# A block kernel whose first modulation third is loaded and multiplied ahead of its token rows

## The chip, the cores and the metric

The kernel runs on one core of a Trainium2 chip, as one program. The metric is its device time in microseconds (us); lower is better. A measurement is several executions, and their median is told.

## The reference, cut to what matters

The program is one layer of a diffusion transformer: 1024 tokens and 256 context tokens of width 1024. A modulation vector of six parts, computed from a conditioning vector, shifts and scales the normed tokens; a mixing block (gated linear attention beside a long convolution, the "hyena" part) and a mixture of 16 experts follow.

```python
mod_x = split((silu(c) @ w_ada + b_ada), N_MOD)            # six parts of 1024
mod_c = split((silu(c_ctx) @ w_ada + b_ada), N_MOD)
def project(h, mod):
    p = (rmsnorm(h, norm_mix_g) * (1 + mod[1]) + mod[0]) @ w_in
    ...
def hyena_filters(L, w1, b1, w2, b2, w3, freq):
    hdn = sin(freq * (z @ w1 + b1)); hdn = sin(freq * (hdn @ w2 + b2))
    h = (hdn @ w3).reshape(L, 2, 2, 512) * exp(-t * deltas)
    ...
x = x + mod_x[2] * merge(gla(project(x)), hyena(project(x), filters))
x = x + mod_x[5] * moe(rmsnorm(x) * (1 + mod_x[4]) + mod_x[3])
return rmsnorm(x, norm_final_g)
```

Parts 0 and 1 of the modulation (the shift and the scale of the first norm) are its first third: without them no token row can be projected.

## The kernel before, in words

The weight matrix w_ada of the modulation is 1024 by 6144. It is taken in three thirds `t` of 2048 columns. Of each third, 16 tiles `wt` of 128 rows by 1024 columns (512 KB) are loaded, and each is multiplied by four matmul instructions in the program (eight on the engine) with a 32-column tile `sc` of the two conditioning vectors (`mod_piece`, L325 to L336). The four write four quarters of 32 partitions of one accumulator `pm`; the sum is added into the tile `mo`, which holds the bias (`mod_begin`, L318 to L324). The two vectors stand in the rows 32 g and 32 g + 1 of `mo`, for the four column groups g. Thirds 1 and 2 are computed much later, among the convolution's slots, and are written to the DRAM tensor `d_mod` (`mod_end`). The first third stays on the chip: four transposes (L349) turn it into per-channel columns `mcol`, and `g1` is its scale with the norm's gain.

The order of the program at the start is this. The features of the filters are computed first: two small layers with sines (`sin_layer`; products L243 and L254, activation L236), with the loads of the filters' output weights `w3raw` ahead of them and a split of each of these into a high and a low part (`split_w3`, ACT L247 and DVE L248). Then come the DFT matrices `fmat` and `fneg`, and the first four tiles of token rows (`rows_of`, 128 rows each): loads of the rows and of the position table's parts (L282, L288, L295), their additions on VectorE (L297, L298), a square on ScalarE for the norm (L300), and the scaling (L305). Then the first third of the modulation, all 16 tiles in one piece. After that `columns` transposes and modulates the rows (L501, L503) into `xh` and `xl`, for the first four row tiles and then for the second four. The second four have the position table added by an accumulating transfer that GpSimd issues (L290), and use the same buffers as the first four. The filters (`filter_front`, products L451 and L452, multiplication L454; `filter_mid`, the transform's products L467 and L468) are eight units without any need of the rows; the projections (`short_conv`, product L542) need both halves of the rows.

What each engine does when is set at build time: a planner takes the instructions in program order as their priority, and puts each on its engine's queue when, by its own estimate, its inputs are there. So the filters' products stand between those of the modulation and of the rows. On the chip each queue is in order. The SyncE queue (SP) issues nearly all loads, also in that order; a load waits where its buffer isn't free. The modulation's tiles of the first third have eight buffers (tag `wa`) in a pool that is closed before the pool of `xh` and `xl` is opened.

## Time and profile before

| | |
|---|---|
| median of 3 runs | 1385.44 us |
| lowest and highest | 1383.4 and 1390.76 us |
| the profiled execution's own time | 1382.24 us |
| its span | 1380.5 us |
| TensorE busy | 1275.1 us |
| VectorE busy | 1149.6 us |

The page gives one execution: engine sums, 40 slices, groups and waits. Engines: PE is TensorE's matmuls, PEld its weight loads, DVE is VectorE, ACT is ScalarE, POOL is GpSimd, SP is SyncE, which only issues transfers. A timeline row has the start in us, the duration, the engine, the line, the operation with its output and inputs, and a count; in brackets, the idle time of the engine before it and what ended it. Where a row counts "x2" or "x8", the duration is that of the whole row. The chain of waits that ended last is followed back only to about 650 us in this profile, so that the start must be read from windows, waits and timelines.

### The profile page before, as it was taken

The page shows a single profiled execution, that of the slowest core. Times are in us where ns is not written, and L with a number is a line of the kernel's source. Part 1 is how long each engine was busy: PE and PEld are TensorE (multiplying, and loading weights), DVE is VectorE, ACT ScalarE, POOL GpSimd, SP SyncE. Part 2 cuts the span into 40 slices and gives each one's busy share as a digit, 9 for nine tenths or more (in the row PEclk, how much of TensorE's full clock was granted, in tenths as well). Part 3 has the DMA queues.
Part 4 walks back from the last instruction along what each step waited for, and adds up shares of the span by engine and source line. Part 5 has one row for each costly group of instructions (what it writes and reads, how often), then busy time and mean ns, then how long its engine had stood idle before and what let it go on. Part 6 is the DMA issues. An engine that isn't in the chain of part 4 may idle for free.

```text
span 1380.5 us, 21546 instructions
## 1 busy us (share of the span) xinstructions
PE 1275.1 (92%) x7720; PEld 1043.0 (76%) x7720; DVE 1149.6 (83%) x1920; ACT 806.4 (58%) x1228; POOL 130.1 (9%) x142
## 2 busy tenths in 40 slices
PE   6978999999999997987996899999999999999982
PEld 4777888687898896766775678888888888877762
DVE  6877838899778778878756799999999999988885
ACT  3247453211221415885553578888888888877864
POOL 1110000010100110000000000011111111012010
PEclk9998999999999998998996799999999999999996
DMA  7893541774655536766668689999999999999765
GB/s 223 315 241 118 177 128 47 229 218 146 187 169 167 154 100 186 176 158 174 221 230 348 241 316 357 358 394 381 395 381 390 385 389 383 372 366 370 265 204 223
DMA packets 154362, 354.81 MB, mean 257 GB/s; under 512 B 28389, under 2 KB 74013, under 8 KB 153999
## 3 DMA queue, kind: packets, MB, share of 16 engines
q1 hardware_dynamic: 134911, 292.84, 59.7%
q0 software_dynamic: 19344, 60.61, 15.7%
q8 instruction: 60, 0.98, 0.3%
q14 instruction: 47, 0.39, 0.1%
HBM read 310.89 MB, written 50.89 MB: 262 GB/s over the span
## 4 chain that ended last, share of the span: by engine, by line
PE 45%; DVE 4%; DMA 2%; issue 1%; ACT 1%; SPq 0%; POOLq 0%; POOL 0%; DVEq 0%; ACTq 0%
PE pex L151 13%; PE pex L152 12%; PE pex L150 12%; PE ptx L1341 2%; DVE elo L147 1%; PE psel L1252 1%; PE pout L150 1%; DMA eraw<-w_up 1%; PE pout L151 1%; DVE xf L1414 1%; PE pout L152 1%; DVE state L635 0%; PE po L1123 0%; PE po L1127 0%; DMA xs<-d_h,ix 0%
## 5 line engine op out<-in xcount | busy, mean ns | idle before, releaser
L147 DVE TENSOR_TENSOR elo<-eraw,ehi 128x1024 fp32r<-128x1024 f32 x256 | 302.5, 1219 | 13.0 <-issue 5.9
L151 PE MATMUL pex<-elo,thi 128*128 128x512 f32 x768 | 306.0, 398 | 4.7 <-DVE elo L147 4.4
L150 PE MATMUL pex<-ehi,thi 128*128 128x512 f32 x768 | 305.4, 398 | 2.3 <-ACT thi L144 1.3
L152 PE MATMUL pex<-ehi,tlo 128*128 128x512 f32 x768 | 303.4, 395 | 0.8 <-DVE tlo L147 0.8
L144 ACT ACTIVATE ehi<-eraw 128x1024 fp32r<-128x1024 f32 x256 | 265.0, 1068 | 50.2 <-PE pex L152 49.3
L151 PEld LDWEIGHTS pex<-elo,thi 128*128 128x128 f32 x768 | 145.2, 189 | 40.4 <-DVE elo L147 10.4
L150 PEld LDWEIGHTS pex<-ehi,thi 128*128 128x128 f32 x768 | 145.2, 189 | 34.1 <-ACT thi L144 1.7
L152 PEld LDWEIGHTS pex<-ehi,tlo 128*128 128x128 f32 x768 | 145.0, 189 | 31.7 <-DVE tlo L147 1.2
L147 DVE TENSOR_TENSOR elo<-erawl,ehi 128x1024 fp32r<-128x1024 f32 x128 | 149.4, 1218 | 6.4 <-ACT ehi L144 5.6
L144 ACT ACTIVATE ehi<-erawl 128x1024 fp32r<-128x1024 f32 x128 | 131.3, 1057 | 19.6 <-PE pex L152 18.0
L144 ACT ACTIVATE whi<-wraw 128x1024 fp32r<-128x1024 f32 x30 | 31.8, 1060 | 104.9 <-DMA wraw<-w_in 28.4
L542 PE MATMUL phy<-xh,whi 128*128 128x512 f32 x192 | 77.2, 402 | 11.3 <-ACT whi L144 11.3
L543 PE MATMUL phy<-xl,whi 128*128 128x512 f32 x192 | 76.0, 396 | 0.0
L150 PE MATMUL pvg<-whi,xh 128*128 128x256 f32 x256 | 73.2, 286 | 0.0
L151 PE MATMUL pvg<-wlo,xh 128*128 128x256 f32 x256 | 72.4, 283 | 0.0
L152 PE MATMUL pvg<-whi,xl 128*128 128x256 f32 x256 | 72.4, 283 | 0.0
L1387 POOL DMA_INDIRECT d_acc<-y,ix x15 | 34.6, 2308 | 392.5 <-DVE y L1386 392.5
L1346 ACT ACTIVATE tt<-ptx,fcol,gfcol 128x128 f32<-128x128 f32 x128 | 48.7, 463 | 33.9 <-PE ptx L1341 33.9
L545 PE MATMUL phy<-xh,wlo 128*128 128x512 f32 x192 | 61.9, 399 | 0.0
L438 ACT ACTIVATE D<-pdft 128x512 f32<-128x512 f32 x32 | 19.1, 597 | 68.9 <-PE pdft L468 39.4
L147 DVE TENSOR_TENSOR wlo<-wraw,whi 128x1024 fp32r<-128x1024 f32 x30 | 36.6, 1221 | 21.2 <-ACT whi L144 21.1
L467 PE MATMUL pdft<-kk,fmat 128*128 128x128 f32 x256 | 52.1, 286 | 0.3 <-ACT D L438 0.2
(452 smaller groups left out, 2596.3 us busy)
## 6 DMA issues: line engine op xcount, KB each, us to landing
eraw<-w_gate SPq DMA_DIRECT2D x128, 512.0 KB
eraw<-w_up SPq DMA_DIRECT2D x128, 512.0 KB
erawl<-w_down SPq DMA_DIRECT2D x128, 512.0 KB
wt<-w_ada SPq DMA_DIRECT2D x48, 512.0 KB
wraw<-w_in SPq DMA_DIRECT2D x30, 512.0 KB
kspec<-d_spec SPq DMA_DIRECT2D x16, 512.0 KB
xt<-x SPq DMA_DIRECT2D x8, 512.0 KB
d_spec<-ue POOLq DMA_DIRECT2D x8, 512.0 KB, 5.9
```

What stands on the lines that cost most here:

```text
L144: A.activation(hi, src, AF.Copy)
L147: V.tensor_sub(lo, src, hi.bitcast(F32))
L150: T.matmul(out_, lh, rh, start=first, stop=False)
L151: T.matmul(out_, lh, rl, start=False, stop=False)
L152: T.matmul(out_, ll, rh, start=False, stop=last)
L467: T.matmul(ps[:, r], fmat[:, r, m1], kk[m1 // 4][:, 0, m1 % 4], start=True, stop=False)
L542: T.matmul(ps[:, h], hi[:, k], rh[k][:, h], start=k == 0, stop=False)
L543: T.matmul(ps[:, h], hi[:, k], rl[k][:, h], start=False, stop=False)
L545: T.matmul(ps[:, h], lo[:, k], rh[k][:, h], start=False, stop=k == KT - 1)
L1341: T.transpose(pt[:, k], src[:, (4 * g + k) * P:(4 * g + k + 1) * P], ident)
L1346: A.activation(tt[:, k], pt[:, k], AF.Identity, bias=fcol[:, 0, kk_:kk_ + 1], scale=gfcol[:, kk_:kk_ + 1])
L1387: G.indirect_dma_start(out=d_acc[:, :], out_offset=bass.IndirectOffsetOnAxis(ap=ix[:, :1], axis=0), in_=y, in_offset=None, compute_op=ALU.add)
```

## The change

The conditioning vector's activation, the helpers of the modulation and the first half of the first third (`mod_piece(0, (0, 1), ...)`, eight tiles) move ahead of the loads of `w3raw`. The second half (`mod_piece(0, (2, 3), ...)`) stays after the second `w3raw` split and the first decay, but now stands ahead of the first token rows, which move behind the transposes of the modulation and `g1`. The first third has 16 buffers instead of eight, so no load of it waits. Since it is two pieces, there are two accumulators and two additions into `mo`. In all three thirds the bias comes in two transfers of four partitions (every 32nd) instead of eight of one, and in the last two the vectors go out in two instead of four.

```diff
     SY.dma_start(ccol[:, :, 1], io["c_ctx"].rearrange("(k p) -> p k", p=P))
+    V.tensor_scalar(fb[:, 3:4], fb[:, 2:3], 1.0 / (2 * math.pi), None, op0=ALU.mult)
+    sc = early.tile([P, KT, 32], F32, name="sc")
+    G.memset(sc, 0.0)
+    A.activation(sc[:, :, 0:2], ccol, AF.Silu)
...
+    def mod_columns(rows, t, i):
+        return rows[i, 2048 * t:2048 * t + 2048].rearrange("(h g j) -> g h j", h=2, g=4)
+
+    def mod_begin(t, pool):
+        mo = pool.tile([P, 512], F32, name="mo", tag="mo", bufs=1)
+        G.memset(mo, 0.0)
+        for i in range(2):
+            SY.dma_start(mo[i::32].rearrange("g (h j) -> g h j", h=2), mod_columns(io["b_ada"], t, 0))
+        return mo
...
+    def mod_end(t, mo):
+        for i in range(2):
+            G.dma_start(mod_columns(d_mod, t, i), mo[i::32].rearrange("g (h j) -> g h j", h=2))
+
+    mo = mod_begin(0, early)
+
+    def wa(shape, name):
+        return wap.tile(shape, F32, name=name, tag="wa", bufs=16)
+
+    mod_piece(0, (0, 1), mo, wa)
 
     w3v = io["hy_w3"][0].rearrange("k (o d c) -> o k d c", o=2, d=2)
...
-    first_rows = rows_of(io["x"][0], 0, 4, True)
...
-    def mod_columns(rows, t, g):
-        return rows[:, 2048 * t:2048 * t + 2048].rearrange("r (h g j) -> r g h j", h=2, g=4)[:, g]
...
-        for g in range(4):
-            for i in range(2):
-                SY.dma_start(mo[32 * g + i:32 * g + i + 1].rearrange("r (h j) -> r h j", h=2), mod_columns(io["b_ada"], t, g))
...
-        for g in range(4):
-            G.dma_start(mod_columns(d_mod, t, g), mo[32 * g:32 * g + 2].rearrange("r (h j) -> r h j", h=2))
...
-    mo = mod_begin(0, early)
-    mod_piece(0, range(4), mo, lambda shape, name: wap.tile(shape, F32, name=name, tag="wa", bufs=8))
+    mod_piece(0, (2, 3), mo, wa)
     gcol = early.tile([P, KT], F32, name="gcol")
...
         V.scalar_tensor_tensor(g1[:, i], mcol[:, i, 1], 1.0, gcol, op0=ALU.add, op1=ALU.mult)
+
+    first_rows = rows_of(io["x"][0], 0, 4, True)
+
     wa_stack.close()
```

## Rows read from the trace of the kernel before

**Rows 1.** The page, its span and the sums of the engines.

```profile
span 1380.5 us, 21546 instructions
...
PE 1275.1 (92%) x7720; PEld 1043.0 (76%) x7720; DVE 1149.6 (83%) x1920; ACT 806.4 (58%) x1228; POOL 130.1 (9%) x142
```

**Rows 2.** Windows: us, busy of PE, PEld, DVE, ACT, POOL, granted clock, DMA share, GB/s.

```profile
0.00:20.60 20.60, 7.89 (x8) 2.16 (x8) 11.97 (x25) 4.96 (x8) 3.29 (x10) 1.00 0.80 223
...
28.00:46.00 18.00, 18.00 (x154) 17.16 (x154) 15.44 (x29) 6.97 (x14) 1.55 (x3) 1.00 0.75 282
46.00:73.50 27.50, 27.50 (x264) 19.48 (x264) 20.16 (x46) 6.06 (x7) 3.73 (x7) 1.00 0.85 256
73.50:95.90 22.40, 22.29 (x192) 21.60 (x191) 22.06 (x52) 12.56 (x21) 6.27 (x9) 1.00 0.90 256
95.90:107.20 11.30, 0.04 (x1) 0.00 (x0) 2.97 (x8) 4.41 (x9) 0.00 (x0) 0.72 0.91 240
107.20:111.00 3.80, 3.76 (x15) 3.57 (x16) 3.68 (x12) 0.66 (x3) 0.54 (x1) 0.50 0.34 138
```

**Rows 3.** Waits of PE, 20 to 200 us: total, times, longest.

```profile
PE phy L542 <- ACT whi L144: 11.3, 1, 11.3
```

**Rows 4.** Timeline, SP's loads of the second rows and ACT's queue behind them.

```profile
82.86 1.85 SPq L288 DMA_DIRECT2D xt<-x  x4
...
105.09 1.06 ACT L300 ACTIVATE jk<-xt 128x1024 bf16<-128x1024 f32 x1 [2.35 <-DMA xt<-c_pos]
...
106.14 1.04 ACT L144 ACTIVATE whi<-wraw 128x1024 fp32r<-128x1024 f32 x1
```

**Rows 5.** DMA queues, 84 to 106 us: packets, MB, share of 16 engines.

```profile
q0 software_dynamic: 892, 3.14, 61.2%
```

**Rows 6.** Timeline of PE, the filters' first products.

```profile
20.65 0.58 PE L451 MATMUL pw<-w,h2h 128*128 128x256 f32 x1 [3.50 <-ACT h2h L266]
...
22.39 0.41 PE L452 MATMUL pw<-w,h2l 128*128 128x256 f32 x1
22.61 0.41 PE L451 MATMUL pw<-w,h2h 128*128 128x256 f32 x1
...
28.16 0.63 PE L467 MATMUL pdft<-kk,fmat 128*128 128x128 f32 x2
...
30.09 0.28 PE L452 MATMUL pw<-w,h2l 128*128 128x256 f32 x1
30.21 0.28 PE L451 MATMUL pw<-w,h2h 128*128 128x256 f32 x1
```

**Rows 7.** Timeline of PE, one piece of the modulation between transform products.

```profile
46.77 0.39 PE L468 MATMUL pdft<-kk,fmat 128*128 128x128 f32 x2
47.08 0.64 PE L334 MATMUL pm<-wt,sc 128*32 128x256 f32 x8
47.65 0.49 PE L467 MATMUL pdft<-kk,fmat 128*128 128x128 f32 x2
47.98 0.39 PE L468 MATMUL pdft<-kk,fneg 128*128 128x128 f32 x2
```

**Rows 8.** Timeline of SP's queue, 0 to 140 us.

```profile
8.14 2.50 SPq L222 DMA_DIRECT2D w3raw<-hy_w  x4
...
24.23 1.28 SPq L323 DMA_DIRECT2D mo<-b_ada  x2
...
31.81 27.22 SPq L332 DMA_DIRECT2D wt<-w_ada  x16
```

**Rows 9.** DMA, 30 to 60 us in 40 slices of 0.75 us.

```profile
GB/s 31 183 139 57 164 246 415 437 366 404 404 421 421 399 388 415 410 404 410 399 137 33 66 218 344 268 246 289 279 246 289 344 415 355 339 322 339 366 393 404
```

**Rows 10.** Timeline of ACT and DVE, the filter weights' first split, and the filters' first multiplication.

```profile
13.46 1.06 ACT L247 ACTIVATE w<-w3raw 128x1024 fp32r<-128x1024 f32 x1 [0.69 <-DMA w3raw<-hy_w]
14.42 0.61 ACT L236 ACTIVATE h<-sy 64x512 f32<-64x512 f32 x1
...
23.71 1.21 DVE L454 TENSOR_TENSOR kk<-pw,decay 128x1024 f32<-128x1024 f32 x1
```

More of the change, by code (lines that the diff above doesn't have):

```diff
@@ L223, in tile_gla_hyena_moe @@
         w3raw.append(raw)
-    V.tensor_scalar(fb[:, 3:4], fb[:, 2:3], 1.0 / (2 * math.pi), None, op0=ALU.mult)
-    sc = early.tile([P, KT, 32], F32, name="sc")
-    G.memset(sc, 0.0)
-    A.activation(sc[:, :, 0:2], ccol, AF.Silu)
     def sin_layer(dst, ps, bcol, rows):
```

29 lines of the change are left out of this document (12 added, 17 removed).

## The prediction

> **What bounds the kernel now.** I read the page first: TensorE is busy for 1275.1 of 1380.5 us, more than any other engine [rows 1]. So a microsecond can be won only where TensorE stands idle, runs at its lower clock, or does work that could be done in such a place. The change touches the first 110 us, so I then cut those into stretches [rows 2]. From 0 to 20.6 us TensorE is busy for 7.89 us only. From 28.0 to 95.9 us it is full: 18.00 of 18.00, 27.50 of 27.50 and 22.29 of 22.40 us. From 95.9 to 107.2 us it does nothing (0.04 us), and from 107.2 to 111.0 us it works at a granted clock of 0.50, the 1.2 GHz level. VectorE is busy for 57.7 of the 67.9 us of the full part, so it is close behind but not the bound.
>
> The list of waits names the hole: the first product of the input projection waits 11.3 us for ScalarE to split a weight block [rows 3]. The timeline shows that the split itself is not what is late [rows 4]. It stands in ScalarE's queue behind the four squares of the second token rows; the last of them starts at 105.09, the split at 106.14. The squares wait for the rows: their loads are issued at 82.86, when the first rows' buffers come free, and then GpSimd adds the position table by an accumulating transfer. In that time GpSimd's transfers take 61.2% of all the transfer engines' time for 3.14 MB [rows 5]. The hole is thus 23 us from the issue of the loads to the last square, less the 13 us of work that TensorE had in its queue (82.86 to 95.9).
>
> At the other end, the filters' first product starts at 20.65, and the first product of their transform at 28.16 [rows 6]. In between the same product starts every 0.22 us (22.39, 22.61); at 30 us it starts every 0.12 us (30.09, 30.21). So this group runs at the lower of the two levels, though the clock column gives 1.00 there; in the hole's aftermath the column and the spacing agree.
>
> **The change, part by part.** The sum is made against the profiled execution (1382.24 us; its span is 1380.5); the median of the runs shown is 3.2 us above it.
>
> *Eight of the 16 products of the modulation leave the full stretch.* Each piece (eight matmuls) comes between transform products: the pair at 46.77 would be followed after 0.22 us, at 46.99; instead the piece starts at 47.08, the next pair at 47.65, and the one after that 0.33 us later instead of 0.22 [rows 7]. That is 0.66 + 0.11 = 0.77 us a piece, 6.2 us for eight. They now run while the filters' features are being computed, where TensorE has 12.7 us free (20.6 less 7.89). Since the stretch that they leave has no idle time: **-6.2 us**. The cover is that free time; if it is not used, this term is nothing.
>
> *The filters' weights now stand behind 4 MB.* SyncE's queue goes by the order of the program as long as nothing waits, and with 16 buffers nothing does. It now issues the filter weights at 8.14, and the bias and modulation loads only from 24 and 31.81 us on [rows 8]. After the change two bias transfers come first (1.28 us, as the two at 24.23), then eight weight tiles, then the filter weights. While the modulation's first eight tiles stream now, the transfers run at 399 to 421 GB/s [rows 9]. Eight tiles and the first filter's weights are 4.19 + 0.52 = 4.72 MB: 11.7 us at 404 GB/s, so from 9.5 to 10 us on they land at about 22 instead of 13.4 (when the split could start). ScalarE's part of the split is 1.06 us and VectorE's about as long as its multiplication of 1.21 us [rows 10], so the filters' product could start at 24.3 instead of 20.65. Yet today that product is held up inside (7.5 us from 20.65 to 28.16, for the second half of its features, a table load and the second filter's split). With all features ready, eight products at 0.215 us, that multiplication of 1.21 us and 0.45 us for the bias row lead to the transform at 27.7; the DFT matrix, 1.57 MB behind, lands at about 26 to 27. So the lower bound of the delay is about nothing. The upper bound: ScalarE's queue holds the split (13.46) ahead of the activation of the first layer's second half, which follows at 14.42 [rows 10]. If that order stays, this activation starts at 23.1 and everything after it is 8.7 us late; the first layer's products can likewise stand behind modulation tiles in TensorE's queue. I take **+1.5 us**: the split has no reason to be put early when its data come late, but one or two modulation tiles ahead of the layer's products are likely.
>
> What row and page make of the rate: [rows 9] show a stretch at over 400 GB/s for a single core. The Trainium skill, "DMA: Bandwidth & Descriptors", Specifications, gives about 358 GB/s as the limit of the HBM side for one core; by it the weights would land 1.5 us later and the term be 3.0 instead of 1.5 us. The measurement decides.
>
> What the rows show of the clock: the filters' first 16 products run at the lower level after an idle stretch [rows 6]. The Trainium skill, "TensorE: Matmul & The Clock Gate", Part 1, says that the low clock is the default and activity releases it; by that the moved products could have the clock up before the filters start, and 16 products at 0.12 instead of 0.22 us would give another 1.6 us. I leave it out of the sum: the modulation products come in bursts.
>
> *The first rows are loaded after the modulation.* Their loads, additions and squares are the same instructions, later. The eight tiles of the second half and the rows (3.4 MB) are issued without waiting and land before 50 us by the same rate. The transposes need both; today they wait for the modulation, whose last load is issued at 59.0 (31.81 + 27.22) [rows 8]. So the transposes, and with them the second rows' loads, come ten or more us earlier. This frees nothing by itself, as TensorE is full then. A new wait is possible: if the first rows' loads land later than the planner thinks, their additions and squares hold the filters' evacuations behind them in VectorE's and ScalarE's in-order queues, and TensorE with them. What is late next is the second rows' chain of 23 us, unchanged: **0**, with -13.1 (hole 11.3 and half of 3.6 us at the low level) and +6 (half a hole of today's kind, before the first squares) as bounds.
>
> *Small parts, all at nothing.* The second half's loads pass only the first rows' on SyncE's queue, and GpSimd's clearing of the bias tile already stands at the start. Six bias transfers fewer a third: SyncE is idle around the later ones. Four vector transfers fewer a third, on GpSimd, which is free 90% of the time [rows 1]. One more VectorE addition of 0.7 us: covered by its 10 us idle in the full stretch; without that cover it costs its 0.7.
>
> Sum: -6.2 + 1.5 = -4.7 us, 1377.5 against the profiled execution; against the median 1385.44 it is **1380.7 us**. By its own bounds (delay of nothing to 7 us, the clock's 1.6) this case reaches from 1377 to 1386.
>
> **The rivals.**
> *The hole closes.* The second rows come earlier, their chain meets fewer other transfers, and TensorE has more filter work queued beside it. For it: some 39% of the transfer engines' time in that window is not GpSimd's [rows 5], and not all of it is the rows' own loads. Against it: the chain is 23 us wherever it stands, ScalarE's queue is in order, and the order is fixed by the same planner. Two thirds of the 13.1 us gone with the forecast's gain: about 1372; all of it: 1367.6.
> *The filters start late.* The one that ends slower. Its place is ScalarE's and TensorE's queues at 10 to 28 us. At the 282 GB/s of the stretch from 28 to 46 us [rows 2] the 4.72 MB land at 26.7 us; with the order of [rows 10] kept, the activation of 14.42 starts at 27.8, and the filters are 13.4 us late: +13.4 - 6.2 = +7.2, 1392.6. It decides when the filter weights land after about 26 us and a step of the feature chain stands behind their split.
> *The change doesn't do what it says.* The planner, which interleaves by its own estimate of the loads, can still put the first half's products between the filters' products; then nothing is won but the delay is paid: 1385 to 1387.
>
> **How the numbers follow.** A measurement can tell about 0.5%, 6.9 us. The forecast's case has 0.45, of which 0.12 lies beyond 0.5% (a small part of the hole goes too, or the clock comes up early). The hole closing to most of it: 0.30. No move: 0.12, within 0.5%. Late filters: 0.13, slower. So faster 0.30 + 0.12 = 0.42, same 0.33 + 0.12 = 0.45, slower 0.13. The likeliest is the forecast. The range leaves out a tenth at each side: from 1366, the hole gone, to 1392, most of the late start.
>
> **What would show it.** In the changed kernel's trace: half of the modulation's 128 matmuls before the filters' first product, none of them between its transform products before the second half; the filter weights' split near 22 to 24 us and the transform's first product at 28 to 31 us. The full stretch should be 6 us shorter, and a hole of 8 to 14 us should still stand before the first projection product, behind the squares of the second rows. Wrong would be: no such hole, a first transform product after 34 us, or waits of TensorE for modulation tiles inside the filters.

## The result, and the profile after

The changed kernel is slower. Its median is 1396.26 us (1394.12 to 1398.36, 5 runs) against 1386.69 us (1383.4 to 1390.76, 5 runs) for the kernel before: a ratio of 1.0063, interval 1.0036 to 1.0089. The forecast was 1380.7 us, and the range ended at 1392. The profiled execution took 1395.03 us with a span of 1393.2.

The page of the changed kernel, the lines that answer to [rows 1]:

```profile
span 1393.2 us, 21484 instructions
...
PE 1282.8 (92%) x7720; PEld 1045.9 (75%) x7720; DVE 1150.4 (83%) x1921; ACT 806.6 (58%) x1228; POOL 127.8 (9%) x138
```

Nothing but VectorE's one addition was added, yet TensorE is busy 7.7 us longer with the same 7720 matmuls, and idle for 5 us more (110.4 against 105.4). More busy time with the same work points to the lower of the clock's two levels (0.50 granted, 1.2 GHz).

The same stretches as in [rows 2], as windows of the changed kernel:

```profile
0.00:20.60 20.60, 6.83 (x28) 1.82 (x28) 3.91 (x11) 1.50 (x2) 3.23 (x10) 1.00 0.77 243
28.00:46.00 18.00, 14.03 (x108) 10.42 (x102) 11.92 (x18) 5.24 (x7) 1.53 (x3) 1.00 1.04 371
46.00:73.50 27.50, 25.12 (x222) 22.29 (x215) 21.37 (x47) 6.28 (x11) 2.24 (x5) 0.98 0.76 176
73.50:95.90 22.40, 19.12 (x142) 17.05 (x141) 20.98 (x46) 16.36 (x27) 3.92 (x7) 0.95 0.46 162
95.90:107.20 11.30, 6.24 (x52) 5.68 (x50) 7.12 (x18) 2.77 (x6) 3.75 (x5) 0.96 1.02 256
107.20:111.00 3.80, 2.50 (x11) 2.50 (x12) 1.29 (x2) 1.25 (x3) 0.00 (x0) 0.50 1.06 285
```

The stretch that was full (28.0 to 95.9) now has 9.6 us of idle time (4.0, 2.4 and 3.3), and the hole behind it is half as long (5.1 of 11.3 us). The list of TensorE's waits from 0 to 200 us, which answers to [rows 3], says what took the hole's place:

```profile
PE pm L244 <- DMA wt<-w_ada: 13.8, 1, 13.8
PE pdft L474 <- ACT D L445: 7.4, 2, 5.9
PE pw L458 <- ACT h2h L305: 4.0, 1, 4.0
PE pw L458 <- DVE kk L461: 3.5, 4, 2.4
...
PE phy L549 <- ACT whi L144: 0.5, 1, 0.5
```

The one wait of 11.3 us for the weight split is down to 0.5, and the time stands in others. Not all of them are new: the kernel before has 12.7 us of idle time up to 20.6 us too, mostly in waits of the feature layers, so the 13.8 us at the start are about 1 us more idle time, in front of other work. I followed the waits one at a time.

**The start.** The timeline of SyncE's queue in the changed kernel (start, duration; compare [rows 8]):

```profile
8.05 1.18 SPq L233 DMA_DIRECT2D mo<-b_ada  x2
9.27 4.31 SPq L242 DMA_DIRECT2D wt<-w_ada  x8
13.65 4.32 SPq L265 DMA_DIRECT2D w3raw<-hy_w  x4
...
23.20 9.43 SPq L242 DMA_DIRECT2D wt<-w_ada  x8
...
38.76 0.43 SPq L327 DMA_DIRECT2D xt<-x  x1
...
89.77 2.48 SPq L327 DMA_DIRECT2D xt<-x  x4
```

The queue does what the prediction said, issuing the tiles ahead of the filter weights (13.65 instead of 8.14). The weights are there at 25.61, when their split starts after a wait of 1.55 us, and not at about 22. TensorE's own timeline, which answers to [rows 6], does not:

```profile
13.77 1.08 PE L244 MATMUL pm<-wt,sc 128*32 128x256 f32 x8 [13.77 <-DMA wt<-w_ada]
14.78 2.07 PE L282 MATMUL pmlp<-zf,w 33*128 33x512 f32 x2
16.78 1.93 PE L244 MATMUL pm<-wt,sc 128*32 128x256 f32 x16
...
27.65 1.93 PE L244 MATMUL pm<-wt,sc 128*32 128x256 f32 x16
33.55 1.10 PE L458 MATMUL pw<-w,h2h 128*128 128x256 f32 x2 [3.98 <-ACT h2h L305]
...
34.67 0.41 PE L458 MATMUL pw<-w,h2h 128*128 128x256 f32 x1
34.88 0.41 PE L459 MATMUL pw<-w,h2l 128*128 128x256 f32 x1
...
38.28 0.28 PE L459 MATMUL pw<-w,h2l 128*128 128x256 f32 x1
38.40 0.28 PE L458 MATMUL pw<-w,h2h 128*128 128x256 f32 x1
...
40.02 0.39 PE L474 MATMUL pdft<-kk,fmat 128*128 128x128 f32 x2
```

The feature layer's products (pmlp), which began at 3.93 before, now stand behind a modulation product that waits until 13.77 for its tile, and then alternate with modulation products. The filters' first product comes at 33.55 instead of 20.65, the transform's at 40.02 instead of 28.16. The filters' first products run at the lower of the clock's levels: they start every 0.21 us around 34.88 and every 0.12 us at 38.28.

**The rows.** ScalarE's queue in the changed kernel, cut to the squares (jk) of both halves of the rows and the evictions (D) of the filters between them; it answers to [rows 4]:

```profile
62.72 1.06 ACT L339 ACTIVATE jk<-xt 128x1024 bf16<-128x1024 f32 x1 [0.95 <-DVE xt L336]
...
68.19 1.06 ACT L339 ACTIVATE jk<-xt 128x1024 bf16<-128x1024 f32 x1 [4.31 <-DVE xt L336]
...
69.59 0.60 ACT L445 ACTIVATE D<-pdft 128x512 f32<-128x512 f32 x1 [0.25 <-DVE vr L387]
72.94 1.06 ACT L339 ACTIVATE jk<-xt 128x1024 bf16<-128x1024 f32 x1 [2.75 <-DVE xt L336]
...
78.46 4.27 ACT L344 ACTIVATE xt<-xt,prs 128x1024 f32<-128x1024 f32 x4 [2.65 <-DVE prs L164]
83.15 1.45 ACT L510 ACTIVATE tt<-pt,mcol,g 128x512 f32<-128x512 f32 x2 [0.42 <-PE pt L508]
...
106.81 1.06 ACT L339 ACTIVATE jk<-xt 128x1024 bf16<-128x1024 f32 x1 [1.84 <-DMA xt<-c_pos]
...
107.87 0.58 ACT L445 ACTIVATE D<-pdft 128x512 f32<-128x512 f32 x1
```

The first rows' squares now fall among the filters' evictions and wait for VectorE's additions. VectorE's eight additions for these rows stand between filter work from 56.32 to 72.9 us. The rows' copies (tt) start at 83.15; in the kernel before they started at 75.99, as soon as the modulation was there. In the changed kernel the modulation is ready at 57 us, and the rows are what is late. From 60 to 90 us TensorE's longest wait is not for an eviction but for VectorE (2.4 us, the filters' multiplication kk). The second rows follow: their loads at 89.77 (82.86 before), and their squares hold an eviction until 107.87, the 5.9 us wait in the list above.

**An account.** To compare kernels whose stalls lie in different places, I summed the trace's windows of 2 us from 0 to 180 us: TensorE's idle time, and its busy time multiplied by (1 minus granted clock). For the kernel before this gives 25.5 + 1.9 = 27.4 us, for the changed kernel 30.8 + 4.0 = 34.8. So 7.4 us of the difference lies there (the spans of these two executions differ by 12.7 us, the medians by 9.6): 4.1 more idle up to 60 us, 3.9 idle and 1.7 at the half clock from 60 to 90, and 2.3 less from 90 to 180. The sum can't see the half pace of the start, where the clock column gives 1.00.

### The profile page after: what moved, and what is told of

Read it like the earlier page. It is cut to its first block, busy times and chain, and to the rows that moved or that the text cites. A ratio compares the mean times of both kernels' runs of the same rounds, so it can differ in the third digit from the quotient of the medians.

```text
span 1393.2 us, 21484 instructions
## 1 busy us (share of the span) xinstructions
PE 1282.8 (92%) x7720; PEld 1045.9 (75%) x7720; DVE 1150.4 (83%) x1921; ACT 806.6 (58%) x1228; POOL 127.8 (9%) x138
## 4 chain that ended last, share of the span: by engine, by line
PE 44%; DVE 4%; DMA 2%; issue 1%; ACT 1%; SPq 0%; POOLq 0%; POOL 0%; DVEq 0%; ACTq 0%
PE pex L151 13%; PE pex L152 12%; PE pex L150 12%; PE ptx L1348 2%; DVE elo L147 1%; PE psel L1259 1%; PE pout L150 1%; DMA eraw<-w_up 1%; PE pout L151 1%; DVE xf L1421 1%; PE pout L152 1%; DVE state L642 0%; PE po L1130 0%; DMA xs<-d_h,ix 0%; PE po L1134 0%
## 5 line engine op out<-in xcount | busy, mean ns | idle before, releaser
L147 DVE TENSOR_TENSOR elo<-eraw,ehi 128x1024 fp32r<-128x1024 f32 x256 | 302.6, 1220 | 13.1 <-issue 6.0
```

What stands on the lines that cost most here:

```text
L147: V.tensor_sub(lo, src, hi.bitcast(F32))
```

## The experiments

The four theories in the order in which they came: the start alone (order on TensorE, or the filter weights behind the tiles); the rows' new place; the merged bias transfers; and the rows' squares in ScalarE's in-order queue as what turns any of these into a stall. Each group of kernels ran beside the kernel before. Its medians in the five groups lay between 1384.6 and 1388.3 us, and its single runs between 1381.5 and 1393.8, so each result is given as a ratio to the runs of its own group, with the 95% interval in brackets. An "eviction" is ScalarE's copy of a transform's result out of TensorE's output buffers (D<-pdft).

### One repair of the start at a time

**e2_psum**: the first third's products in another PSUM tag than the feature layers' (both use two buffers of one tag).

```diff
-        pm = pB([P, 512], name="pm")
+        pm = (pC if t == 0 else pB)([P, 512], name="pm")
```

> The changed kernel, with the accumulator of the first third in another PSUM tag, so that it shares no buffers with the feature layers' products. Theory A (the products of the modulation came ahead of the feature layers on TensorE's queue because both take buffers of one tag, and held the features up): the first layer's products start at about 4 us instead of 14.8, its activation at about 12 instead of 21.9; the filters' first product then waits for the filter weights and starts near 29 to 30 instead of 33.5, and the time falls by 3 to 5 us against the changed kernel, to about 1392. Theory B (the filter weights behind 4 MB are what is late): the features come early but the filters' first product moves by under 1 us, the time by under 1 us. Theory C (the later place of the first rows costs the time): no change of the time over 2 us.

Measured: 1399.71 us, 1.0096 (1.0068 to 1.0125). The feature layers do go first again, and all 64 matmuls of the modulation's first half run before the filters, in the free time that the prediction meant. But the filters' first product is still at 30.09 and the transform's at 37.67. ScalarE's queue of e2 shows the hold that is left:

```profile
26.00 1.06 ACT L286 ACTIVATE w<-w3raw 128x1024 fp32r<-128x1024 f32 x1 [11.95 <-DMA w3raw<-hy_w]
26.96 1.13 ACT L275 ACTIVATE h<-sy 128x512 f32<-128x512 f32 x2
```

The second layer's activation, whose inputs VectorE had finished at 20.3 and 21.4 us, stands behind the split of the filter weights, which land at 26.00. This is the rival "the filters start late" as the prediction described it.

**e3_w3_first**: the filters' last weights loaded ahead of the modulation.

```diff
     mo = mod_begin(0, early)
...
-    mod_piece(0, (0, 1), mo, wa)
...
     w3v = io["hy_w3"][0].rearrange("k (o d c) -> o k d c", o=2, d=2)
...
             SY.dma_start(raw[r:r + 64], w3v[o])
         w3raw.append(raw)
...
+    mod_piece(0, (0, 1), mo, wa)
```

> The changed kernel, with the filter weights' loads ahead of the modulation's. Theory A: the modulation's tiles come 2 to 3 us later, and the feature layers with them; the filters' first product at 34 to 36 us, the time the same to 3 us more than the changed kernel's, 1396 to 1399. Theory B: the first product comes at 25 us or so and the time falls by 5 to 9 us. Theory C: no change.

Measured: 1400.37 us, 1.012 (1.0086 to 1.0153); the transform starts at 39.45. The run doesn't clear the late weights, though: the modulation's tiles now come later, TensorE's first product waits for one until 18.11 instead of 13.77, and the feature layers still stand behind it. The start has two holds, one behind the other: the features behind the tiles on TensorE, which e2 lifts, and the features behind the weights on ScalarE, which e3 lifts. Either repair leaves the other hold.

**e4_rows_back**: the first rows again ahead of the modulation's second half.

```diff
+    first_rows = rows_of(io["x"][0], 0, 4, True)
     mod_piece(0, (2, 3), mo, wa)
...
-    first_rows = rows_of(io["x"][0], 0, 4, True)
```

> The changed kernel, with the first token rows back ahead of the modulation's second half. Theory A and theory B: the first 35 us stay as they are (filters' first product at 33.5), the time within 2 us of the changed kernel's 1396. Theory C: stalls between 60 and 111 us (12 us of TensorE idle in the changed kernel) shrink to under 8 us and the time falls by 4 us or more.

Measured: 1395.2 us, 1.0078 (1.0052 to 1.0105). No gain by itself.

**c2_late_w3first**: weights first as in e3, the tiles loaded early, and their products put in the program behind the feature layers.

```diff
-    mod_piece(0, (0, 1), mo, wa)
...
+    ahead_wt = iter([[load_wt(0, k, h, wa) for h in range(2)] for k in range(4)])
...
+    mod_piece(0, (0, 1), mo, wa, ahead_wt)
     tc.keep_in_program_order(A.preload_act_table_set("natural_log_exp_and_others"))
```

> The changed kernel, with the filter weights' loads first and the first half's products traced behind the feature layers (its loads stay ahead). If theories A and B together hold the whole loss: the features and the filters' first product as in the kernel before (20.7 us), the first transform product at about 28 us, time 1384 to 1387 as before, less what the moved products give. If theory C holds a part: the start as before, but the time still above that of the kernel before by 2 us or more.

Measured: 1398.7 us, 1.0103 (1.0076 to 1.0129). With both holds lifted the filters' first product is at 19.87, but the transform comes only at 35.82. TensorE doesn't stand for it (12.8 us idle up to 60 us, 13.7 in the kernel before); other products come first in its order, among them the 64 matmuls of the modulation's first half, which now stand between the filters' products.

No one of these repairs brings the time back. The next group put the start's order back as a whole and split the change the other way, from the kernel before.

### The whole start, the rows, the merge

**c6_filter_loads_first**: c2, with the transform's matrices and the identity loaded ahead too.

```diff
...
+    fmat = cload("fmat", [P, 2, 8, P], pool=cp)
+    fneg = cp.tile([P, 8, P], F32, name="fneg", tag="fi0")
+    SY.dma_start(fneg, io["c_fneg"])
+    ident = cload("ident", [P, P])
...
```

> The changed kernel, with all loads of the filters (their weights, both DFT matrices, the identity) ahead of the modulation's, and the first half's products traced behind the feature layers. Four repairs of one late input at a time left the time at 1395 to 1400 us; in each the first transform product still stood at 36 to 40 us instead of 28. Theory D (the first transform product must come early, whatever holds it: queue order, weights or DFT matrix; VectorE has nothing to do in the meantime and has too much later): it starts at 28 to 30 us, VectorE is busy for 14 us or more of the 18 from 28 to 46 us, and the time falls to 1384 to 1389. Theory E (it is the late first rows: 5.4 us of VectorE additions, eight of them, and four squares stand between 56 and 75 us instead of 26 to 43): the start is repaired and the time stays above 1392.

Measured: 1398.29 us, 1.0087 (1.0059 to 1.0115), with the transform at 28.63, within 0.5 us of the kernel before. An early start alone is worth nothing here. It also gives the change's gain away, as TensorE's timeline of c6 shows:

```profile
27.42 1.05 PE L249 MATMUL pm<-wt,sc 128*32 128x256 f32 x8
```

This is the first product of the modulation: none of the 64 matmuls now runs in the free time before the filters' first product (19.78), and they stand among the transform's products again, as in the kernel before. The same holds for c7 (first one at 27.65).

**c7_c6_rows_back**: c6 with the first rows ahead of the modulation's second half, as in e4.

> The kernel of c6 with the first rows back ahead of the modulation's second half. Theory D: as c6 within 2 us. Theory E: 5 us or more below c6, to 1386 or less. If both it and c6 stay above 1392, the cause is neither.

Measured: 1387.5 us, 1.0007 (0.9984 to 1.003): level with the kernel before, 10.8 us below c6. So the rows' place counts, but only once the start is right (e4 alone gave nothing). With the products back in the full stretch and the rows back in their place, c7 is in the main the change undone, apart from the merge, the 16 buffers, the two pieces and the place of some loads.

**b4_rows_behind_16**: the kernel before, with only the first rows behind the modulation and its 16 buffers.

```diff
-    first_rows = rows_of(io["x"][0], 0, 4, True)
...
-    mod_piece(0, range(4), mo, lambda shape, name: wap.tile(shape, F32, name=name, tag="wa", bufs=8))
+    mod_piece(0, range(4), mo, lambda shape, name: wap.tile(shape, F32, name=name, tag="wa", bufs=16))
...
+    first_rows = rows_of(io["x"][0], 0, 4, True)
     wa_stack.close()
```

> The kernel before, with only the first rows moved behind the modulation and 16 buffers; nothing stands ahead of the filters. Theory D: the start stays (first transform product at 28 us) and the time stays within 3 us of the kernel before, 1382 to 1388. Theory E: the rows' work falls into VectorE's full stretch and the time rises by 5 us or more, to 1390 or above.

Measured: 1393.95 us, 1.0046 (1.0028 to 1.0063). The rows' place alone, with the buffers that it needs, costs 6.4 us. Between 60 and 90 us TensorE's idle time rises from 0.1 to 3.9 us, and its longest wait there is 2.6 us for VectorE's multiplication kk, which stands behind the rows' additions.

**e5_bias_only**: the kernel before, with only the bias and the vectors of all thirds moved in two transfers each.

```diff
...
-        for g in range(4):
-            for i in range(2):
-                SY.dma_start(mo[32 * g + i:32 * g + i + 1].rearrange("r (h j) -> r h j", h=2), mod_columns(io["b_ada"], t, g))
+        for i in range(2):
+            SY.dma_start(mo[i::32].rearrange("g (h j) -> g h j", h=2), mod_columns(io["b_ada"], t, 0))
...
-        for g in range(4):
-            G.dma_start(mod_columns(d_mod, t, g), mo[32 * g:32 * g + 2].rearrange("r (h j) -> r h j", h=2))
+        for i in range(2):
+            G.dma_start(mod_columns(d_mod, t, i), mo[i::32].rearrange("g (h j) -> g h j", h=2))
```

> The kernel before, with only the bias and the vectors in a quarter and a half of the transfers. All theories: no difference that can be measured, within 3 us of the kernel before; a difference would say that the bias transfers' place in the load queue matters.

Measured: 1395.64 us, 1.0057 (1.0037 to 1.0076). The part that the prediction set at nothing costs 7.9 us by itself, nearly as much as the whole change. The trace says where. SyncE's queue of e5:

```profile
24.09 1.22 SPq L322 DMA_DIRECT2D mo<-b_ada  x2
25.36 1.16 SPq L295 DMA_DIRECT2D posr<-c_posr  x2
26.56 1.07 SPq L331 DMA_DIRECT2D wt<-w_ada  x2
```

The bias loads stood right ahead of the modulation's tiles, so the first tile is issued at 26.56 instead of 31.81 [rows 8]. The modulation's products are added to the bias at 69.73 instead of 73.65, and in the planner's order the first rows' copies now stand earlier in ScalarE's queue. In the kernel before, four filter evictions stand between the rows' scaling and the copies; the first and the last of them are

```profile
53.90 0.60 ACT L438 ACTIVATE D<-pdft 128x512 f32<-128x512 f32 x1 [3.35 <-PE pdft L468]
...
74.92 0.60 ACT L438 ACTIVATE D<-pdft 128x512 f32<-128x512 f32 x1 [5.27 <-PE pdft L468]
75.99 1.69 ACT L503 ACTIVATE tt<-pt,mcol,g 128x512 f32<-128x512 f32 x2 [0.47 <-DVE g L356]
```

In e5 two do (57.47 and 64.10). ScalarE's queue of e5:

```profile
64.10 0.60 ACT L437 ACTIVATE D<-pdft 128x512 f32<-128x512 f32 x1 [6.03 <-PE pdft L467]
72.42 1.54 ACT L502 ACTIVATE tt<-pt,mcol,g 128x512 f32<-128x512 f32 x2 [7.72 <-DVE g L355]
...
92.61 1.06 ACT L300 ACTIVATE jk<-xt 128x1024 bf16<-128x1024 f32 x1 [7.26 <-DMA xt<-c_pos]
...
95.82 1.06 ACT L300 ACTIVATE jk<-xt 128x1024 bf16<-128x1024 f32 x1 [2.06 <-DMA xt<-c_pos]
...
99.64 1.06 ACT L300 ACTIVATE jk<-xt 128x1024 bf16<-128x1024 f32 x1 [2.68 <-DMA xt<-c_pos]
...
100.70 0.58 ACT L437 ACTIVATE D<-pdft 128x512 f32<-128x512 f32 x1
```

ScalarE waits 7.72 us for the modulation with nothing to do, and a filter eviction that is now left over stands behind three squares of the second rows until 100.70. TensorE's timeline of e5 at that point:

```profile
90.97 0.39 PE L467 MATMUL pdft<-kk,fneg 128*128 128x128 f32 x2
101.33 0.80 PE L466 MATMUL pdft<-kk,fmat 128*128 128x128 f32 x2 [9.97 <-ACT D L437]
```

In the kernel before it was a weight split that stood there, and VectorE had filter work to go on with (12.36 us busy from 90 to 111 us); in e5 the filters themselves stop (8.47 us). TensorE then runs at a granted clock of 0.50 from 102 to 108 us, has a second stop from 123.4 to 127.4, and 0.50 again behind it. By the account above: 30.3 + 6.5 = 36.8 us, 9.4 more than before.

### Is it the squares in ScalarE's queue?

The first three kernels leave the position table out of the second four rows, so that their squares wait for no accumulating transfer; part of the computation is missing. Ahead of the copies the order of ScalarE's queue stays as it was (four evictions in the kernel before, two in e5). The fourth kernel undoes the merge in the changed kernel.

```diff
-    columns(rows_of(io["x"][0], 1, 4, True, True), 1, 0, xh, xl)
+    columns(rows_of(io["x"][0], 1, 4, False), 1, 0, xh, xl)
```

**g_nopos_before** (on the kernel before):

> The kernel before, with the position table left out of the second four token rows (no accumulating transfers by GpSimd; the second rows are then plain x, so part of the computation is missing). Theory F (the time is lost where the second rows' squares stand in ScalarE's in-order queue and wait for those transfers, with an eviction or a weight split of the filters and the projection behind them): the 11.3 us hole of before goes nearly whole, and the half-clock stretch behind it; median 1371 to 1379 us. Theory G (the hole is only where work that is late anyway shows, and DVE or the filter chain sets the end): 1383 to 1388.

Measured: 1382.79 us, 0.9969 (0.9952 to 0.9986). The wait for the weight split is gone, but only 4.3 us are won; 5.0 us of a new wait for an eviction appear. The median lies outside theory F's range and 0.2 us below theory G's, so on the kernel before the expectation of theory F fails.

**g_nopos_e5** (on the merge alone):

> The kernel with only the bias and vector transfers merged, and the position table left out of the second rows in the same way. Theory F: the 8 us that the merge alone cost came from what the squares hold up, so this kernel stands within 4 us of the kernel before with the same left out. Theory G (the merge's own transfers, or the order of the rest, cost the time): it stays 6 to 10 us above it.

Measured: 1385.69 us, 0.9987 (0.9969 to 1.0006). It stands 2.9 us above g_nopos_before, instead of 7.9, within theory F's 4 us: most of what the merge costs goes through the second rows' squares, as far as the intervals of some 2.5 us to either side of each tell. The waits for evictions fall from 15.0 to 5.2 us.

**g_nopos_after** (on the changed kernel):

> The changed kernel, with the position table left out of the second rows in the same way. Theory F: within 6 us of the kernel before with the same left out (the first transform is 12 us late here, of which the start's own idle time of PE, 4 us more, cannot go). Theory G: it stays 9 to 12 us above it.

Measured: 1394.37 us, 1.0057 (1.0038 to 1.0076), 11.6 us above g_nopos_before. Here theory F falls: in the changed kernel the waits of the second rows' squares are not what costs.

**i_after_unmerged** (the changed kernel with eight bias loads and four vector stores a third):

> The changed kernel with the bias and the vectors moved in eight and four transfers as before. If the merged transfers themselves cost what the merge alone cost (8 us): 1387 to 1390 us. If the merge only shifts the planner's order by its prices and the loss is the stalls' (theory F): anything from 1386 to 1400, with the profile's stalls and half-clock stretches up to 180 us adding up to the difference from before.

Measured: 1402.75 us, 1.0122 (1.0085 to 1.0159), above both expectations, and the account up to 180 us gives only 10.3 of the 16.9 us. In the changed kernel the merge helps: with six transfers more ahead of the tiles, TensorE's first product starts at 17.1 instead of 13.8 us. The same edit costs 7.9 us in one kernel and saves 6 to 8 in the other (6.5 by the medians, 8 by the ratios of the two groups), so it has no price of its own.

### The merge, in halves, and the rows' squares again

**p_late_vec**: the kernel before with the merge in all but the first third's bias loads.

```diff
...
-        for g in range(4):
-            for i in range(2):
-                SY.dma_start(mo[32 * g + i:32 * g + i + 1].rearrange("r (h j) -> r h j", h=2), mod_columns(io["b_ada"], t, g))
+        for i in range(2) if (t > 0) else ():
+            SY.dma_start(mo[i::32].rearrange("g (h j) -> g h j", h=2), mod_rows(io["b_ada"], t, 0))
...
-            G.dma_start(mod_columns(d_mod, t, g), mo[32 * g:32 * g + 2].rearrange("r (h j) -> r h j", h=2))
+            G.dma_start(mod_rows(d_mod, t, i), mo[i::32].rearrange("g (h j) -> g h j", h=2))
```

> The kernel before, with the bias loads of the second and third thirds and the stores of all vectors merged, the first third's eight bias loads kept. Theory H (the merge costs time only because the first third's weights are then issued six transfers earlier, which moves the first rows' transposes ahead of two filter evictions): the order up to the second rows is that of before, 1384 to 1389 us. Rival (merged transfers across four partition rows are themselves slow or late): 1391 us or more.

Measured: 1389.08 us, 1.0022 (1.0002 to 1.0042), 0.1 us above theory H's range, and below e5. The interval leaves a cost of 0.3 to 5.8 us, so these parts are not shown to be free. The account up to 180 us is 28.4, 1.0 more than before: these parts leave the first rows alone.

**q_early_pad**: the kernel before with the first third's bias merged and six small loads put back among the tiles.

```diff
...
+        for i in range(2) if (t == 0) else ():
+            SY.dma_start(mo[i::32].rearrange("g (h j) -> g h j", h=2), mod_rows(io["b_ada"], t, 0))
...
+    mo = mod_begin(0, early); pad = [SY.dma_start(early.tile([1, 128], F32, name="pad"), io["b_ada"][:, 0:128]) for _ in range(6)]
```

> The kernel before with only the first third's bias loads merged (two transfers for eight), and six small loads into spare tiles put between the weights' loads. The order of ScalarE's queue has three filter evictions ahead of the first rows' copies, where before has four and the merge alone has two. Theory H: between the two, 1387 to 1395 us. If the number of transfers by itself mattered: 1385 to 1388. If the merged form did: as the merge alone, 1394 to 1397.

Measured: 1384.79 us, 0.9992 (0.9976 to 1.0008). With useless loads in the queue, the time is that of the kernel before: 2.2 us below the range of theory H, 0.2 us below that of the rival that goes by the number of transfers, and far from that of the merged form. This kernel also keeps the later thirds' transfers unmerged; the first third's merge without the loads was not run by itself. ScalarE's queue of q_early_pad shows the difference to e5:

```profile
71.60 0.60 ACT L438 ACTIVATE D<-pdft 128x512 f32<-128x512 f32 x1 [8.69 <-PE pdft L468]
74.70 1.55 ACT L503 ACTIVATE tt<-pt,mcol,g 128x512 f32<-128x512 f32 x2 [2.50 <-DVE g L356]
...
93.81 1.06 ACT L300 ACTIVATE jk<-xt 128x1024 bf16<-128x1024 f32 x1 [6.17 <-DMA xt<-c_pos]
...
94.86 0.58 ACT L438 ACTIVATE D<-pdft 128x512 f32<-128x512 f32 x1
```

Three evictions instead of two stand ahead of the copies, and the next one stands behind one square (94.86), not behind three (100.70). The merged form of the first third's bias loads is thus not at fault. That the order is fits both traces, but the time alone doesn't tell it from the number of transfers, which sets the order here.

**g_noboth_after**: the changed kernel without the position table in the first and in the second rows (no additions, no accumulating transfers; part of the computation is missing).

```diff
-    first_rows = rows_of(io["x"][0], 0, 4, True)
+    first_rows = rows_of(io["x"][0], 0, 4, False)
...
```

> The changed kernel with the position table left out of the first and of the second four token rows (no table loads, no adds on VectorE, no accumulating transfers; the rows are plain x, so part of the computation is missing). Theory J (in the changed kernel the FIRST rows' squares, now among the filters' evictions at 58 to 73 us, stall ScalarE's queue as well, 8 us behind VectorE's adds): some 5 to 8 us below the same kernel with the table left out of the second rows alone, 1386 to 1390 us. Rival (the start alone, PE's first work at 13.8 us and the filters 12 us late, makes the loss): 1392 to 1395.

Measured: 1391.12 us, 1.0058 (1.0033 to 1.0083). The median lies between the two expectations, but by the ratio nothing is won over g_nopos_after (1.0057), so theory J isn't borne out by the time. The account is: up to 180 us it is 28.8, only 1.4 above the kernel before and 5.8 below g_nopos_after, so the first rows' stalls are smaller; but TensorE's idle and half-clock time between 180 and 800 us is 72.9 us, where the kernel before has 64.0 and e5 65.1. That doesn't locate the loss, since q_early_pad (73.4) and g_nopos_c7 (72.7) have as much there and are not slow. Why this kernel keeps its loss is open.

**g_nopos_c7**: c7 without the second rows' table.

> The changed kernel with the filter's loads ahead of the modulation's, its first products traced behind the feature layers and the first rows back ahead of the modulation's second half, and the position table left out of the second rows. Theory F and J (with start and first rows repaired, what is left is the second rows' squares): 1381 to 1386 us, level with the kernel before without that table (1382.8). If something else of the change costs time: 1388 or more.

Measured: 1382.21 us, 0.9974 (0.9958 to 0.9991), level with g_nopos_before. With start and rows put back, nothing of the change is left to pay, and nothing of its gain is seen either.

### A kernel that computes everything

**h_dvepos_before** and **h_dvepos_c7**: the second rows' table added by VectorE, as for the first rows, in the kernel before and in c7.

```diff
-    columns(rows_of(io["x"][0], 1, 4, True, True), 1, 0, xh, xl)
+    columns(rows_of(io["x"][0], 1, 4, True), 1, 0, xh, xl)
```

> The kernel before, with the second four rows' position table added by VectorE (eight adds of 0.67 us, as for the first rows) and no accumulating transfers. Leaving the table out gave 5.4 us; the adds are 5.4 us of VectorE. Theory F (what counts is that ScalarE's queue no longer waits for GpSimd's transfers): 1381 to 1386 us, a little below before. Rival (VectorE has no room there, so the adds hold the evictions up instead): 1387 to 1392.

> The changed kernel with start and first rows repaired as in the run that stood level with before, and the second rows' table added by VectorE in the same way. Theory F: 1381 to 1386 us. Rival (VectorE has no room): 1387 to 1392.

Measured: on the kernel before 1383.36 us, 0.9974 (0.9959 to 0.9989), a small gain over the kernel before, within theory F's range. The largest wait left in its list of TensorE's waits from 30 to 182 us is this one, in place of 11.3 us:

```profile
PE phy L542 <- DVE kk L454: 4.1, 1, 4.1
```

On c7: 1392.6 us, 1.0039 (1.002 to 1.0057): theory F misses; the range of the rival (VectorE has no room) ends 0.6 us below the time. There VectorE is full from 90 to 120 us (29.89 of 30 us, 19.88 in c7), and 8.9 us of waits for evictions remain. So the same cure helps in one order and hurts in another.

### All runs by the account

TensorE's idle time and half-clock loss up to 180 us, worked out from the 2 us windows as above, beside the kernel before's 27.4, and the measured difference ((ratio - 1) x 1386.7 us):

```
kernel             idle  clock   sum  against before  measured
after              30.8   4.0   34.8       +7.4         +8.7
e2_psum            34.8   9.6   44.4      +17.0        +13.3
e3_w3_first        35.3   2.6   37.9      +10.5        +16.6
e4_rows_back       30.3   5.4   35.7       +8.3        +10.8
c2_late_w3first    31.6   8.1   39.7      +12.3        +14.3
c6_filter_loads    33.3   4.8   38.1      +10.7        +12.1
c7_c6_rows_back    26.7   2.7   29.4       +2.0         +1.0
b4_rows_behind_16  30.9   2.8   33.7       +6.3         +6.4
e5_bias_only       30.3   6.5   36.8       +9.4         +7.9
i_after_unmerged   33.8   3.9   37.7      +10.3        +16.9
p_late_vec         26.7   1.7   28.4       +1.0         +3.1
q_early_pad        22.7   3.2   25.9       -1.5         -1.1
g_nopos_before     21.5   1.5   23.0       -4.4         -4.3
g_nopos_e5         23.3   5.9   29.2       +1.8         -1.8
g_nopos_after      30.4   4.2   34.6       +7.2         +7.9
g_noboth_after     27.3   1.5   28.8       +1.4         +8.0
g_nopos_c7         21.8   1.4   23.2       -4.2         -3.6
h_dvepos_before    21.2   3.4   24.6       -2.8         -3.6
h_dvepos_c7        29.0   1.7   30.7       +3.3         +5.4
```

Sixteen of the nineteen agree within 4 us. Two of the others (e3, i_after_unmerged) have the slow start, whose half pace this sum doesn't see; that this explains them is not shown, since the changed kernel and e4 have such a start too and agree. The third is g_noboth_after. So what separates most of these kernels is how long TensorE stands or runs at half clock in the first 180 us. The table can't be read more finely than some 4 us: each sum comes from one execution, and those of the kernel before and of q_early_pad lie 4.5 us below and above their medians; from 180 to 800 us the same sum goes from 64 to 74 us without following the time.

That the second rows' squares ahead of a filter eviction make the loss is shown for e5 in the main (against g_nopos_e5, with q_early_pad beside it). For the first rows (b4, c6 against c7) only their place is shown to cost: it moves VectorE's additions as well as ScalarE's squares, and TensorE's longest waits from 60 to 90 us are there for VectorE's kk (2.6 us in b4, 3.7 in c6, 1.6 in c7). For the changed kernel itself the squares' part is read from its trace, and the experiments that took the squares' waits away alone did not bring its time back. A rival is left for it: up to 60 us VectorE has done 29.1 us of work, against 43.7 in the kernel before, and this backlog may make the later stalls. No run separates the two.

## Why the prediction was wrong

The steps that failed are the cover of the one gain (the free time at the start), the delay of the filters, set at 1.5 us, and the rows' new place, set at nothing. With the start and the rows put back (c7) the loss is gone; either alone leaves it.

**What bounds the kernel: right.** TensorE's idle time decides, and the hole was read correctly down to the squares in ScalarE's queue. What was missed is that the hole's length is not a property of the second rows' chain. It depends on what happens to stand behind the squares, and how much of the filters is left to do then.

**"Eight of the 16 products leave the full stretch: -6.2 us."** They left: 64 of the 128 matmuls ran before the filters' first product. But the term was a gain only if the free time at the start stayed free for the features. The products went ahead of the features instead, waiting 13.8 us for their tiles, and at the lower level they take 0.97 us a piece (1.93 us for 16 matmuls) instead of the 0.77 of the full stretch. TensorE's idle time up to 60 us rose from 13.7 to 17.8 us. There is a second gap in the step: the full stretch ends in the hole, and in the kernel before the hole ends when the second rows' squares do, so less work ahead of it saves time only if those rows come earlier too. Their loads came 6.9 us later (89.77 for 82.86). No run shows the 6.2 us: where the products did run in the free time (e2) the filters were late for another reason, and c7, which is level, has them back in the full stretch.

**"The filters' weights stand behind 4 MB: +1.5 us" (bounds 0 to 8.7).** The transform came 11.9 us late, outside the bounds (and the prediction's own range took the delay as 7 at most). It named both holds, the features behind the split on ScalarE and behind the tiles on TensorE, but gave the second no price, and this one was the larger in the changed kernel: the features waited for the first tile until 13.77. The first was there too: the weights landed at 25.61 instead of about 22, since the rate of 404 GB/s wasn't there over the whole way (59 GB/s from 9 to 11 us, 236 from 23 to 25), and in e2 the split held the features from 21.4 to 26.96. Weights first alone (e3) left the transform at 39.45; only with products and matrices put back as well (c6) did it return to 28.63. And the forecast treated the delay as time: c6 has the early transform and is still 1.0087.

**"The first rows are loaded after the modulation: 0" (-13.1 to +6).** Alone it costs 6.4 us (b4), just past the upper bound. The prediction had named the mechanism as "a new wait" (additions and squares ahead of the filters' work) and priced it as half a hole; in b4 3.8 us of the cost lie there, in idle time from 60 to 90 us. The statement that the transposes come ten or more us earlier was wrong: the copies came 7.2 us later (83.15 for 75.99), since the squares ended at 74 us and the modulation, at 57, no longer mattered. Nor did all of the rows' loads come before 50 us: the last two of the position table are issued at 59.26.

**"Small parts, all at nothing."** On the kernel before the merge costs 7.9 us by itself, so nothing was the wrong price. It is not what made the changed kernel slow, though: c7 keeps the merge and is level, and without the merge (i_after_unmerged) the changed kernel is slower still. "SyncE is idle around the later ones" fits the second and third thirds, where 3.1 us (0.3 to 5.8) were measured (p_late_vec), but the first third's eight bias loads stand directly ahead of the tiles [rows 8]. Their 5 us were on the path of the modulation's arrival, and an earlier arrival moved the first rows' copies ahead of two evictions.

**The rivals.** The outcome is slower, and nearest in time to "the filters start late" (1392.6), with a delay of 12 us for the 13.4 given. Its mechanism was there, but behind a larger hold: the weights' split did wait for its load (1.55 us, until 25.61), and in e2 it alone held the features; loading the weights first (e3) left the features behind the tiles. "The hole closes" happened literally (0.5 us left of 11.3), and won nothing, since the time stood elsewhere. The prediction had named a transform after 34 us and the absence of the hole as signs that it was wrong; both are seen.

**What stays open.** The parts do not add: start and rows repaired one at a time gave nothing, together 8 us (c7 against the changed kernel, by the ratios); the merge costs 7.9 us in one kernel and saves 6 to 8 in another. How the planner gets from an earlier arrival to another order was only seen in three orders (four, three and two evictions ahead of the copies). The runs show that the stalls make the time; they give no rule by which a planner's order can be foretold from an edit. Whether ScalarE's squares or VectorE's backlog make the changed kernel's stalls, why g_noboth_after keeps its loss, and why the table on VectorE hurts c7, are not settled.

## What to carry to other kernels

Where a planner writes the order, "a few transfers fewer" is not a small part: ask which arrival it moves, and what the planner will put earlier because of it. Look in every in-order queue for instructions that wait for a transfer with other engines' work behind them (here the squares), since any re-ordering is paid there. Filling idle time of the bound engine helps only if the filler stands behind what the next stage waits for, and if nothing else ends the stretch that it leaves; and before believing the price of one part, run that part alone and the whole without it.

## What the runs showed of the hardware that was not expected

The granted clock has its own tail behind a stall: in e5 TensorE stood from 91 to 101 us, and the column gave 0.50 until past 108 us, so that a stop of 10 us cost 3.7 us more at the half clock. The half-clock part of the sums above is 1.4 to 9.6 us. At the start of a kernel the column gives 1.00 while the products' spacing (0.21 against 0.12 us) shows the lower level: it went up only at about 37.6 us in the changed kernel, although TensorE had been busy with modulation and feature products from 13.8 to 29.6 us (15.75 of 15.8 us). In e2, where 48 matmuls of the modulation follow one another from 18.13 us, it did rise before the filters: the eight at 23.75 take 0.64 us, as in the full stretch. Then TensorE stood until 30.09, and the filters' first products ran at 0.50 all the same, every 0.21 us until 36. What makes the difference isn't separated by these runs. The 1.6 us that the prediction left out for an early rise of the clock were rightly left out for this kernel.
